# Reciprocal roots of six late norm groups: one power operation on GpSimd in place of eight VectorE steps

## The chip, the cores and the metric

The kernel runs on one core of one Trainium2 chip. The metric is the device time of one execution in microseconds (us). Executions of one kernel mostly agree within about 1%. Some are over 1.5% slower than the fastest of the same kernel, at a lower granted TensorE clock; those are called slow, and only fast runs are compared below: ratios are of fast runs alone, while a time quoted with a ratio is the median of all runs.

## The reference

Eight batches of twelve heads, sequence 512, head size 64, in float32. Rows of Q and K are divided by their norms, the scores by tau = 0.1, and then comes a softmax and the product with V.

```python
Q_norm = Q / (np.linalg.norm(Q, axis=-1, keepdims=True) + 1e-10)
K_norm = K / (np.linalg.norm(K, axis=-1, keepdims=True) + 1e-10)
scores = np.einsum('bhqd,bhkd->bhqk', Q_norm, K_norm) / tau
weights = np.exp(scores - np.max(scores, axis=-1, keepdims=True))
weights = weights / (np.sum(weights, axis=-1, keepdims=True) + 1e-10)
return np.einsum('bhqk,bhkd->bhqd', weights, V).astype(np.float32)
```

## The kernel before

The 96 heads are worked off as 48 pairs. For each pair GpSimd squares Q and K (`SQ`), sums of squares are made by TensorE and VectorE (`SSQ`, `RED`), reciprocal roots are made for a group of up to two pairs (`NEW`), Q is scaled on VectorE and K mostly on GpSimd (`SCL`), TensorE transposes (`TR`), VectorE moves the result into `qt` (`EVA`), TensorE makes the scores (`SCO`), ScalarE takes their exponentials (`EXP`, four per pair), TensorE multiplies by V (`PV`), and VectorE divides (`RCP`, `NRM`). GpSimd also converts V to bf16 (`VC`). From group 3 on, group g holds pairs 2g-3 and 2g-2.

Every engine works through a fixed list.

The roots of groups 3 to 25 take eight small VectorE steps: a first guess by integer arithmetic on the float's bits, then two rounds of improvement. The sums `xg` lie in PSUM (`n_ps`):

```python
steps = [
    lambda e: e.tensor_scalar(
        out=yg.bitcast(i32), in0=xg.bitcast(i32), scalar1=-0.5, scalar2=MAGIC,
        op0=ALU.mult, op1=ALU.add),
    yx, yyx, up(yg, 0, 2 * m), yx, yyx, up(rq_g, 0, m), up(rk_g, m, 2 * m)]
```

The squares, which the last experiments alter:

```python
P.add(("SQ", s, 0), "pool", "sq", due_sq(s), [("LD", s, 0), ("LD", s, 1)] + reds_,
      lambda e: e.tensor_tensor(out=sqf, in0=data, in1=data, op=ALU.mult))
```

Of the kernel before, what the change touches and what calls it, by code (L numbers as in the profile page):

```python
# [3 lines left out]
ALU = mybir.AluOpType  # L4
# [102 lines left out]
def bass_cosine_similarity_attention_kernel(  # L107
# [13 lines left out]
    f32, bf16, i32 = mybir.dt.float32, mybir.dt.bfloat16, mybir.dt.int32  # L121

    R_QK, R_V, R_SQ, R_QN, R_QT, R_ET, R_O, R_X = 18, 6, 6, 3, 3, 3, 8, 3

    def sb(name, shape, dt):
        return nc.alloc_sbuf_tensor(name, shape, dt)
# [11 lines left out]
    xs = {g: sb(f"xs{g}", [128, 64], f32) for g in NORM_ON_ACT}  # L138
# [3 lines left out]
    eps = sb("eps", [128, 1], f32)  # L142
    warm_in = sb("warm_in", [128, SEQ], bf16)
# [34 lines left out]
    P.add("eps", "pool", "sm_pool", -98.5, [], lambda e: e.memset(eps[:, :], 1e-19))  # L178
    P.add("table", "act", "table", -900, [], lambda e: e.preload_act_table_set("natural_log_exp_and_others"))
# [95 lines left out]
    def pair(s):  # L275
# [44 lines left out]
        acts = g in NORM_ON_ACT  # L320
# [31 lines left out]
        if s == first[g] and g in NORM_ON_ACT:  # L352
# [6 lines left out]
            P.add(("NEW", g, 6), "dve", "new", TF - 2.6, [("NEW", g, 7), ("NRMS", 0, 0, 1)],  # L359
                  lambda e: e.tensor_copy(out=n_ps[:, g % R_X, 128 : 128 + 2 * m], in_=xs[g][:, 0 : 2 * m]))  # L360
# [136 lines left out]
NORM_ON_ACT = {0: -90, 1: -45, 2: 0.5}  # L497
EARLY = 4
# [15 lines left out]
def slack(s, most):  # L514
    return most * min(1.0, s / 12)
# [4 lines left out]
        "7 8 64 65 103 104 142 143 186 11 187 221 220 105 66 263 262 296 339 338 222 297 264 372 144 188 298 373 720 "  # L520
        "679 415 830 416 417 449 450 102 491 492 374 525 63 340 526 451 721 601 493 602 645 261 754 568 567 873 831 141 "
        "949 185 797 1103 644 219 603 527 678 1137 1060 371 950 295 755 569 1102 1179 646 796 874 680 984 1289 832 1026 "
        "1025 798 907 908 909 337 875 722 1213 490 983 1366 414 448 524 1255 756 1332 1059 1104 951 1136 1442 1254 1288 "
        "1441 1061 1483 1561 985 566 1178 1331 677 1138 1365 1212 600 643 1027 1408 1407 1560 1214 753 1595 1518 829 "
        "1290 1180 719 1594 1636 1713 1671 872 1256 795 1519 1058 1517 1409 1637 1788 1670 906 1333 1484 1101 1367 982 "
        "1443 1823 948 1024 1485 1638 1562 1822 1789 1177 1596 1135 1712 1746 1330 1747 1364 1406 1672 1287 1714 1253 "
        "1211 1516 1824 1748 1635 1790 1559 1482 1669 1440 1593 1745 1711 1787 1821 1864 1865 "
    ),
    "pool": (
        "4 0 1 2 14 27 22 67 35 107 145 50 189 223 89 128 265 341 299 248 172 206 282 237 324 271 375 418 313 347 452 "  # L530
        "494 528 435 358 401 424 511 477 604 466 570 500 723 647 542 681 576 833 553 630 757 587 653 799 706 664 876 "
        "695 729 910 952 771 893 740 859 816 805 1028 882 782 1062 935 986 1105 924 958 1088 1139 1164 1257 1011 1034 "
        "1000 1181 969 1045 1334 1122 1215 1317 1240 1198 1111 1368 1153 1187 1410 1291 1229 1444 1263 1486 1427 1563 "
        "1274 1340 1520 1382 1416 1639 1351 1673 1469 1393 1458 1597 1546 1503 1656 1492 1715 1569 1749 1791 1825 1698 "
        "1611 1580 1645 1687 1721 1622 1774 1763 1732 1808 1797 1839 1851 "
    ),
    "dve": (
        "5 13 15 26 28 19 32 24 21 70 72 34 75 78 109 111 76 114 115 80 117 147 149 119 190 192 150 151 55 152 153 154 "
        "56 155 61 226 157 156 62 158 159 161 224 163 266 195 100 268 101 227 193 94 228 95 229 197 230 302 231 139 232 "
        "140 234 233 133 235 134 342 239 300 344 269 303 177 304 178 305 183 306 184 307 273 308 378 309 211 310 311 "  # L540
        "212 419 376 315 421 253 379 217 380 218 381 345 382 254 383 259 384 260 386 385 349 387 388 287 455 390 288 "
        "453 392 495 497 293 456 294 457 329 458 330 459 422 460 529 461 335 463 426 336 462 363 531 464 364 498 369 "
        "468 370 571 573 406 532 605 533 407 534 412 535 502 536 413 537 440 607 539 538 441 540 446 574 447 544 648 "
        "650 482 608 682 609 483 610 724 611 488 578 612 489 613 684 516 615 614 517 616 617 619 522 651 523 621 558 "
        "726 758 685 559 834 564 686 800 687 565 688 655 689 592 760 690 593 598 692 691 599 693 727 877 697 802 641 "
        "761 635 762 636 763 764 765 642 766 731 767 768 769 669 911 836 670 675 773 676 803 879 711 837 712 838 839 "
        "953 840 717 841 718 842 844 843 846 807 845 880 745 913 746 751 848 752 1063 850 955 787 914 788 915 793 916 "
        "794 917 918 919 987 921 920 884 922 821 989 822 827 956 828 926 1029 864 1031 990 865 991 870 992 993 871 994 "
        "1140 995 960 996 997 998 898 904 1065 899 905 1258 1106 1032 1002 1108 1066 940 1067 941 1068 946 1069 947 "
        "1070 1036 1071 1182 1072 1073 1075 974 1074 1142 975 1077 1335 1109 980 1079 981 1184 1016 1216 1143 1017 1144 "  # L550
        "1145 1146 1022 1113 1147 1023 1148 1150 1149 1050 1218 1151 1051 1369 1056 1155 1057 1185 1260 1219 1093 1220 "
        "1221 1099 1094 1222 1223 1100 1189 1224 1225 1226 1227 1292 1127 1133 1294 1128 1261 1134 1231 1445 1169 1337 "
        "1295 1170 1296 1297 1175 1298 1411 1299 1176 1300 1265 1301 1302 1203 1304 1371 1303 1204 1209 1306 1210 1487 "
        "1308 1413 1372 1245 1373 1246 1374 1338 1375 1251 1376 1252 1377 1378 1379 1342 1414 1380 1285 1279 1286 1280 "
        "1447 1564 1384 1521 1489 1322 1448 1323 1449 1450 1451 1328 1452 1329 1453 1418 1454 1455 1456 1490 1356 1523 "
        "1357 1640 1362 1460 1363 1398 1566 1399 1674 1524 1525 1598 1526 1527 1404 1528 1405 1529 1530 1494 1531 1432 "
        "1532 1600 1433 1533 1438 1535 1716 1439 1537 1642 1474 1475 1601 1602 1567 1480 1603 1604 1605 1481 1606 1571 "
        "1607 1608 1609 1643 1676 1508 1509 1613 1750 1514 1515 1718 1551 1677 1678 1679 1680 1557 1681 1682 1558 1683 "
        "1684 1552 1647 1685 1792 1585 1752 1586 1826 1591 1592 1689 1794 1627 1753 1628 1754 1755 1719 1756 1633 1757 "
        "1634 1758 1723 1760 1661 1662 1667 1759 1761 1668 1765 1795 1828 1829 1703 1830 1831 1832 1709 1704 1833 1710 "  # L560
        "1834 1836 1835 1799 1837 1737 1743 1744 1738 1841 1779 1785 1786 1780 1813 1814 1819 1820 1856 1857 1862 1863 "
    ),
    "pe": (
        "6 -256 -256 -256 -256 -256 -256 23 20 -256 -192 69 71 36 33 -128 42 38 108 43 39 110 79 46 77 48 146 148 81 "
        "116 118 83 51 52 53 54 191 85 57 58 59 87 60 225 120 90 122 96 97 124 160 162 126 91 98 99 164 267 92 93 166 "
        "196 168 135 136 137 138 194 170 301 129 130 198 131 132 200 179 180 181 182 202 236 238 204 173 343 240 174 "
        "175 176 242 272 270 244 207 208 209 210 246 377 274 213 214 215 216 276 312 249 250 314 278 251 252 420 280 "
        "316 348 255 256 257 318 258 346 320 283 284 285 322 289 290 286 454 350 291 389 292 352 391 325 326 354 327 "
        "328 496 356 393 425 331 395 359 332 333 360 397 334 361 423 399 362 530 427 365 366 467 429 367 465 368 431 "
        "402 403 404 433 405 572 408 469 409 410 501 471 411 499 473 436 437 438 439 606 475 442 443 444 503 445 505 "  # L570
        "541 543 478 507 479 480 481 649 509 575 484 545 485 486 547 512 487 577 549 513 514 515 683 551 518 519 520 "
        "579 521 581 554 618 555 556 583 620 557 725 585 560 561 622 654 562 563 624 588 652 589 626 590 591 759 628 "
        "594 595 596 597 656 658 631 632 633 637 660 638 696 694 634 662 639 801 640 698 700 728 665 666 730 702 667 "
        "671 672 704 668 835 732 770 673 674 772 734 707 708 736 709 710 878 713 738 714 804 774 715 716 741 776 742 "
        "778 806 743 747 780 744 912 748 808 749 847 750 810 783 784 785 786 812 849 954 814 789 790 791 851 792 883 "
        "853 881 817 823 855 824 825 818 819 857 826 820 988 885 925 887 860 861 923 889 862 863 1030 891 866 867 868 "
# [63 lines left out]
```

## Time and profile before

| | before |
|---|---|
| time, median of 2 runs | 192.68 us (192.58 to 192.77) |
| span of the profiled run | 189.4 us |
| VectorE (DVE) busy | 169.6 us, 90% |
| GpSimd (POOL) busy | 155.1 us, 82% |
| ScalarE (ACT) busy | 182.5 us, 96% |

From the page of before: the busy times, then three rows of the view that cuts the span into 40 slices (each digit is the busy share in tenths; PEclk is TensorE's granted clock), and the chain of waits by engine.

```profile
span 189.4 us, 6755 instructions
PE 173.9 (92%) x2729; PEld 110.3 (58%) x2729; DVE 169.6 (90%) x593; ACT 182.5 (96%) x211; POOL 155.1 (82%) x144
...
ACT  4799999999999999999999999999999999999993
POOL 5799899999999989999999978849999994516300
PEclk9999999999999999999999999999999999999999
...
ACT 93%; PE 3%; DVE 1%; POOL 1%; ACTq 0%; issue 0%; POOLq 0%
```

The exponentials are the chain. In order of time, one piece of it (start, length, what) covers nearly everything:

```profile
11.28 173.87 ACT et L445 x190
```

The recorded durations of neighbouring exponentials overlap, so ScalarE's real holds have to be read from their starts. In the trace two 128x1024 exponentials start 903 or 904 ns apart at best; I take 903.5. Over the 188 steps of the 189 large ones this makes 169.86 us; 172.26 us pass. ScalarE is held up for 2.4 us in all. I call that sum "holds" below.

### The profile page before, as it was taken

The page shows a single profiled execution, that of the slowest core. Times are in us where ns is not written, and L with a number is a line of the kernel's source. Part 1 is how long each engine was busy: PE and PEld are TensorE (multiplying, and loading weights), DVE is VectorE, ACT ScalarE, POOL GpSimd, SP SyncE. Part 2 cuts the span into 40 slices and gives each one's busy share as a digit, 9 for nine tenths or more (in the row PEclk, how much of TensorE's full clock was granted, in tenths as well). Part 3 has the DMA queues.
Part 4 walks back from the last instruction along what each step waited for, and adds up shares of the span by engine and source line. Part 5 has one row for each costly group of instructions (what it writes and reads, how often), then busy time and mean ns, then how long its engine had stood idle before and what let it go on. Part 6 is the DMA issues. An engine that isn't in the chain of part 4 may idle for free.

```text
span 189.4 us, 6755 instructions
## 1 busy us (share of the span) xinstructions
PE 173.9 (92%) x2729; PEld 110.3 (58%) x2729; DVE 169.6 (90%) x593; ACT 182.5 (96%) x211; POOL 155.1 (82%) x144
## 2 busy tenths in 40 slices
PE   5989999989999999999999899998999989999983
PEld 2645656556665665666656566565666656566552
DVE  2689999999999999999999999989999999987843
ACT  4799999999999999999999999999999999999993
POOL 5799899999999989999999978849999994516300
PEclk9999999999999999999999999999999999999999
DMA  5999999999999699999989944992249940139343
GB/s 159 349 354 349 349 350 374 363 368 370 380 383 305 177 327 374 381 351 362 378 298 295 359 162 154 316 375 84 77 144 358 290 161 21 45 106 283 111 166 111
DMA packets 52302, 50.76 MB, mean 268 GB/s; under 512 B 3120, under 2 KB 52272, under 8 KB 52272
## 3 DMA queue, kind: packets, MB, share of 16 engines
q1 hardware_dynamic: 51984, 50.08, 80.3%
q8 instruction: 21, 0.34, 0.7%
q10 hardware_dynamic: 288, 0.26, 0.4%
q14 instruction: 9, 0.07, 0.1%
HBM read 37.75 MB, written 12.58 MB: 266 GB/s over the span
## 4 chain that ended last, share of the span: by engine, by line
ACT 93%; PE 3%; DVE 1%; POOL 1%; ACTq 0%; issue 0%; POOLq 0%
ACT et L445 93%; PE ops L185 2%; PE scps L188 1%; DVE ob L476 0%; POOL vb L180 0%; ACT qt L265 0%; PE ops L330 0%; ACT ys L355 0%; ACTq L85 0%; ACT xs L357 0%; PE scps L256 0%; PE ops L459 0%; DVE rd L474 0%; POOL ident L175 0%; DVE xs L337 0%
## 5 line engine op out<-in xcount | busy, mean ns | idle before, releaser
L445 ACT ACTIVATE et<-scps 128x1024 bf16<-128x1024 f32 (+1 forms) x195 | 176.5, 1156 | 0.0
L313 POOL TENSOR_TENSOR sq<-qk 128x1024 bf16<-128x1024 f32 x45 | 84.7, 1893 | 4.6 <-DMA qk<-in_K_dram 3.6
L429 PE MATMUL scps<-qt 64*128 64x512 bf16 x384 | 75.4, 385 | 9.0 <-ACT et L445 5.3
L459 PE MATMUL ops<-vb,et 128*128 128x65 bf16 x1536 | 78.3, 194 | 0.8 <-ACT et L445 0.8
L459 PEld LDWEIGHTS ops<-vb,et 128*128 128x128 bf16 x1536 | 58.6, 98 | 29.6 <-issue 21.3
L389 POOL TENSOR_TENSOR qn<-qk,rk 128x512 bf16<-128x512 f32 x37 | 38.3, 1043 | 9.6 <-DVE rk L367 6.5
L476 DVE TENSOR_TENSOR ob<-ops,rd 128x256 f32<-128x256 f32 x96 | 39.5, 415 | 0.4
L389 DVE TENSOR_TENSOR qn<-qk,nps 128x512 bf16<-128x512 f32 x57 | 38.0, 675 | 0.1
L395 PE MATMUL tps<-ident,qn 128*128 128x128 bf16 x376 | 35.1, 220 | 0.7 <-POOL qn L389 0.5
L429 PEld LDWEIGHTS scps<-qt 64*128 64x128 bf16 x384 | 19.4, 93 | 26.8 <-ACT et L445 10.2
L402 DVE COPY qt<-tps 128x1024 bf16<-128x1024 bf16 x47 | 32.2, 685 | 3.1 <-PE tps L395 1.9
L450 POOL TENSOR_SCALAR vb<-vf 128x512 bf16<-128x512 f32 x48 | 29.3, 626 | 5.6 <-DMA vf<-in_V_dram 4.4
L341 DVE TENSOR_REDUCE nps<-sq 128x8 f32<-128x512 bf16 x44 | 29.8, 681 | 0.0
L395 PEld LDWEIGHTS tps<-ident,qn 128*128 128x128 bf16 x376 | 21.7, 98 | 11.7 <-issue 5.9
L474 DVE RECIPROCAL rd<-ops 128x4 f32<-128x4 f32 x96 | 16.6, 175 | 6.3 <-PE ops L459 5.2
L330 PE MATMUL ops<-sq,ident 128*128 128x64 bf16 x400 | 19.7, 193 | 0.0
L330 PEld LDWEIGHTS ops<-sq,ident 128*128 128x128 bf16 x400 | 14.9, 98 | 3.4 <-issue 2.3
L337 DVE TENSOR_REDUCE nps<-ops 128x8 f32<-128x64 f32 x46 | 9.9, 217 | 1.0 <-PE ops L330 0.9
L362 DVE TENSOR_TENSOR nps<-nps,ys 128x32 f32<-128x32 f32 (+1 forms) x46 | 8.8, 191 | 0.3
L363 DVE SCALAR_TENSOR_TENSOR nps<-nps,ys 128x32 f32<-128x32 f32 (+1 forms) x46 | 8.7, 190 | 0.3
L185 PE MATMUL ops<-warm_in,ident 128*128 128x512 bf16 x8 | 3.6, 631 | 2.0 <-POOL eps L178 2.0
L367 DVE SCALAR_TENSOR_TENSOR nps<-nps,ys 128x16 f32<-128x16 f32 (+1 forms) x30 | 5.1, 171 | 0.1
(43 smaller groups left out, 36.2 us busy)
## 6 DMA issues: line engine op xcount, KB each, us to landing
vf<-in_V_dram SPq DMA_DIRECT2D x48, 256.0 KB, 6.0
qk<-in_Q_dram SPq DMA_DIRECT2D x47, 256.0 KB, 6.0
qk<-in_K_dram SPq DMA_DIRECT2D x47, 256.0 KB, 6.1
out_dram<-ob SPq DMA_DIRECT2D x47, 256.0 KB, 5.1
qk<-in_K_dram ACTq DMA_DIRECT2D x2, 128.0 KB, 2.9
qk<-in_Q_dram SPq DMA_DIRECT2D x2, 128.0 KB, 2.7
out_dram<-ob SPq DMA_DIRECT2D x2, 128.0 KB, 1.7
```

The source lines that it names most:

```text
L313: lambda e: e.tensor_tensor(out=sqf, in0=data, in1=data, op=ALU.mult))
L330: last = e.matmul(out=o_ps[bank][:, 320:384], lhsT=ident[:, :], rhs=sq[iqs][:, 8 * w : 8 * w + 8, 8 * k : 8 * k + 8], start=(k == 0), stop ...
L341: lambda e, w=w, dst=dst: e.tensor_reduce(out=dst, in_=sq[iqs][:, 8 * w : 8 * w + 8, :], axis=AX.X, op=ALU.add))
L389: lambda e, w=w, r=r: e.tensor_tensor(out=qn[iqn][:, w].rearrange("p t h d -> p h t d"), in0=qk[iq][:, w].rearrange("p h (t d) -> p h t d" ...
L395: last = e.transpose(t_ps[:, w, t, :], qn[iqn][:, w, t].rearrange("p h d -> p (h d)"), ident[:, :])
L402: lambda e: e.tensor_copy(out=qt[iqt][:, :, :, :].rearrange("p w t x -> p (w t x)"), in_=t_ps[:, :, :, :].rearrange("p w t x -> p (w t x)")))
L429: last = e.matmul(out=sc_ps[:, 2 * b + h, :], lhsT=qt[iqt][64 * h : 64 * h + 64, 1, c, :], rhs=qt[iqt][64 * h : 64 * h + 64, 0, :, :], sta ...
L445: lambda e, c=c, b=b, hs=hs: e.activation(out=et[iet][:, c, hs[0] : hs[-1] + 1, :], in_=sc_ps[:, 2 * b + hs[0] : 2 * b + hs[-1] + 1, :], f ...
L450: lambda e: e.tensor_scalar(out=vb[:, iq, :, :, 0:DIM].rearrange("p c h d -> p h c d"), in0=vf[iv][:, :, :].rearrange("p h (c d) -> p h c ...
L459: last = e.matmul(out=o_ps[h][:, 65 * t : 65 * t + 65], lhsT=et[iet][:, c, h, 128 * t : 128 * t + 128], rhs=vb[:, iq, c, h, :], start=(c = ...
L474: lambda e, h=h, grid=grid: e.reciprocal(out=rd[io][:, h, :], in_=grid[:, :, DIM]))
L476: lambda e, h=h, grid=grid: e.tensor_tensor(out=ob[io][:, h], in0=grid[:, :, 0:DIM], in1=rd[io][:, h, :].unsqueeze(2).to_broadcast([128, N ...
```

## The change

It is meant to relieve VectorE: for six late groups the sums go to SBUF, GpSimd adds a tiny constant and raises to the power -0.5, and VectorE only copies the result into PSUM. The orders of all engines and of the DMA queue were searched anew. The core of the diff:

```diff
-    xs = {g: sb(f"xs{g}", [128, 64], f32) for g in NORM_ON_ACT}
+    xs = {g: sb(f"xs{g}", [128, 64], f32) for g in (*NORM_ON_ACT, *NORM_ON_POOL)}
+    mhalf = sb("mhalf", [128, 1], f32)
+    P.add("half", "pool", "sm_pool", -97, [], lambda e: e.memset(mhalf[:, :], -0.5))
-        acts = g in NORM_ON_ACT
+        acts = g in NORM_ON_ACT or g in NORM_ON_POOL
+        elif s == first[g] and g in NORM_ON_POOL:
+            P.add(("NEW", g, 0), "pool", "sm_pool", TF - 5.8 - slack(s, M_NEW), reds,
+                  lambda e: e.tensor_scalar(
+                      out=xs[g][:, 0 : 2 * m], in0=xs[g][:, 0 : 2 * m], scalar1=1e-19, scalar2=1.0, op0=ALU.add, op1=ALU.mult))
+            P.add(("NEW", g, 7), "pool", "pow", TF - 5.5 - slack(s, M_NEW), [("NEW", g, 0), "half"],
+                  lambda e: e.tensor_tensor(
+                      out=xs[g][:, 0 : 2 * m], in0=xs[g][:, 0 : 2 * m], in1=mhalf[:, :].to_broadcast([128, 2 * m]), op=ALU.pow))
+            P.add(("NEW", g, 6), "dve", "new", TF - 2.9 - slack(s, M_NEW), [("NEW", g, 7), *free[0], *free[1]],
+                  lambda e: e.tensor_copy(out=n_ps[:, g % R_X, 128 : 128 + 2 * m], in_=xs[g][:, 0 : 2 * m]))
+NORM_ON_POOL = (11, 14, 17, 20, 23, 24)
...  # ORDER: every engine's list replaced
```

## The prediction

> **What bounds it now.** ScalarE. In the chain that ended last, the exponentials (L445) hold 92.6%; one unbroken piece of 190 runs from 11.28 us for 173.87 us. The page shows ACT idle 0.0, but recorded durations overlap (median 1168 ns), so I read starts from the trace: neighbouring 128x1024 exponentials start 903.5 ns apart at best (median 904). From first to last start of the 189 large ones 172.26 us pass; 188 steps at 903.5 ns would need 169.86. So ScalarE is held up for only 2.4 us in all, about 1.2 us of it after 72 us, where the changed groups lie. VectorE is busy 169.6 us (90%), GpSimd 155.1 us (82%); neither matters to the chain between 12 and 185 us. By windows, GpSimd is nearly full until 108 us, busy 8.9 to 9.8 of 12 us from 108 to 132, full to 156, and 5.2 to 5.5 of 12 us from 156 to 180.
>
> **The change.** Groups 11, 14, 17, 20, 23, 24 each drop eight VectorE steps on at most 128x32 (188, 192, 191, 183, 192, 191, 172, 161 ns in the groups view: 1.47 us) and gain one copy (like L360, 0.18 us): 6 x 1.29 = 7.7 us off VectorE, 90% to 86%. Sums of squares go to SBUF, since GpSimd cannot access PSUM (the Trainium skill, "GPSIMD Engine Reference", section 1; this trace agrees: no GpSimd line touches a PSUM tile). GpSimd gains an add of about 0.15 us and a power per group. All orders, DMA too, are re-searched.
>
> **Cost of the power.** The trace doesn't measure it, no page states it. Section 3.1 of that page has long GpSimd bodies bound at about 3 operations per cycle; some 50 operations on 32 elements would be about 0.5 us, a dependent chain several us. The diff allows 2.6 us between the power's due time and the copy's. My estimate: 2.3 us, plausibly 0.8 to 6. Six cost 14 us: GpSimd goes to about 170 us.
>
> **Critical path.** Before, roots are ready 2.4 to 3.1 us after the last sum for these groups (1.8 for group 23), since the steps interleave with other VectorE work. Add plus power plus copy with semaphores: about 2.8 us. So latency is unchanged, and VectorE's relief can be cashed only in the 1.2 us of late ScalarE holds. I expect 0.2 to 0.5 us gained there, as much won or lost by the new order elsewhere. Slack before harm: from the copy into qt (L402) to its pair's first exponential 0.8 to 2.4 us (about 0.6 needed), and from scaling to that copy 1 to 3 us. A power above roughly 4.5 us would use this up and stall in-order VectorE at the copy; each excess us would cost up to 6 us in all.
>
> **Predicted time** 192.5 us, 191.4 to 195.0. Faster by over 2% (below 188.8) is practically impossible: removing every ScalarE hold gives about 190.3. Chances 0.01, 0.87, 0.12.
>
> **What would show it.** Exponentials still above 92% of the chain, 903.5 ns start to start, holds summing to 1.5 to 3 us; VectorE busy 162 us, GpSimd 170 us; power group x6 at 2.3 us; first exponential within 0.3 us of 9.27.
>
> **What would make it wrong.** A power far longer than 2.3 us, or a code load at first use: then holes between exponentials in pairs 19, 25, 31, 37, 43, 45, with VectorE waiting at the new copy. A re-searched DMA order that starves GpSimd's squares. Contention of GpSimd and VectorE on SBUF; the trace shows none now (square 1889 to 1902 ns throughout).

## More of the kernel before

The order is a table of numbers, and before each entry the engine waits on semaphores for what that entry needs. So whatever stands behind a waiting entry waits too:

```python
for o in order[name]:
    ... # collect the highest value wanted of each semaphore
    for k, (sem, val) in want.items():
        engine.wait_ge(sem, val)
    inst = o.emit(engine)
    if o.sem is not None:
        inst.then_inc(o.sem, o.inc)
```

The groups of instructions that the change and the argument touch (busy us, mean ns of one, then idle time of the engine before them and its releaser):

```profile
L445 ACT ACTIVATE et<-scps 128x1024 bf16<-128x1024 f32 (+1 forms) x195 | 176.5, 1156 | 0.0
L313 POOL TENSOR_TENSOR sq<-qk 128x1024 bf16<-128x1024 f32 x45 | 84.7, 1893 | 4.6 <-DMA qk<-in_K_dram 3.6
L429 PE MATMUL scps<-qt 64*128 64x512 bf16 x384 | 75.4, 385 | 9.0 <-ACT et L445 5.3
L362 DVE TENSOR_TENSOR nps<-nps,ys 128x32 f32<-128x32 f32 (+1 forms) x46 | 8.8, 191 | 0.3
L363 DVE SCALAR_TENSOR_TENSOR nps<-nps,ys 128x32 f32<-128x32 f32 (+1 forms) x46 | 8.7, 190 | 0.3
```

The small steps of the roots take some 0.19 us each by duration; a square takes ten times that.

## The result

The change took 220.09 us (two runs, 220.05 and 220.14) against 192.68 us: a ratio of 1.1423, 95% interval 1.1374 to 1.1472. Results are correct.

The same views of the page of after:

```profile
span 217.9 us, 6727 instructions
PE 186.2 (85%) x2729; PEld 117.3 (54%) x2729; DVE 166.4 (76%) x551; ACT 185.2 (85%) x211; POOL 189.2 (87%) x157
...
ACT  4799999998999965999579993799947999466993
POOL 4799989879999999999999979997999799989100
PEclk9999999999999996999769997699976999769999
...
ACT 40%; PE 24%; POOL 21%; DMA 6%; DVE 5%; issue 2%; SPq 2%; ACTq 0%; POOLq 0%
...
L456 ACT ACTIVATE et<-scps 128x1024 bf16<-128x1024 f32 (+1 forms) x195 | 179.2, 1086 | 25.5 <-PE scps L440 25.1
L440 PE MATMUL scps<-qt 64*128 64x512 bf16 x384 | 79.2, 405 | 10.3 <-ACT et L456 5.2
L315 POOL TENSOR_TENSOR sq<-qk 128x1024 bf16<-128x1024 f32 x45 | 84.6, 1895 | 3.4 <-DMA qk<-in_K_dram 2.2
L368 POOL TENSOR_TENSOR xs<-xs,mhalf 128x32 f32<-128x32 f32 x6 | 32.6, 5429 | 0.2
L371 DVE COPY nps<-xs 128x32 f32<-128x32 f32 x6 | 1.2, 195 | 20.1 <-POOL xs L368 20.1
```

Read it from the bottom. One power on 128x32 takes 5.43 us (5426 to 5437 ns for all six, the first included), and VectorE stands idle for 20.1 us in front of the six copies. ScalarE's row has five dents, the last of them long and from two powers, and the clock's row falls to 6 or 7 tenths in the same five places. Those are means over slices of 5.4 us: the windows view gives a granted clock of 0.50 from 82.5 to 85.8 us and again from 106.4 to 113.1 us, and 1.00 between. The holds, from the starts of the exponentials, are 30.6 us instead of 2.4. The chain is no longer ScalarE's alone.

The first power in the timeline of after (start, length, engine, line, operation; in brackets the idle time before and its releaser). The cuts are of GpSimd, VectorE, TensorE and ScalarE, in this order, in the same stretch:

```profile
74.58 0.22 POOL L365 TENSOR_SCALAR xs<-xs 128x32 f32<-128x32 f32 x1
74.88 0.63 POOL L461 TENSOR_SCALAR vb<-vf 128x512 bf16<-128x512 f32 x1
75.47 5.44 POOL L368 TENSOR_TENSOR xs<-xs,mhalf 128x32 f32<-128x32 f32 x1
...
80.94 0.20 DVE L371 COPY nps<-xs 128x32 f32<-128x32 f32 x1 [3.48 <-POOL xs L368]
...
78.08 0.39 PE L440 MATMUL scps<-qt 64*128 64x512 bf16 x2 [0.43 <-ACT et L456]
...
81.91 0.40 PE L406 MATMUL tps<-ident,qn 128*128 128x128 bf16 x4 [3.21 <-DVE qn L400]
82.72 0.61 PE L440 MATMUL scps<-qt 64*128 64x512 bf16 x2
...
83.36 1.02 ACT L456 ACTIVATE et<-scps 128x1024 bf16<-128x1024 f32 x1 [3.50 <-PE scps L440]
```

The wait is handed from queue to queue. VectorE stops at the copy for 3.48 us; TensorE stops at the transposes of pair 19, which stand in its list ahead of the last scores of pair 18; ScalarE runs dry for 3.50 us. Then the same two score products take 0.61 us instead of 0.39.

### The profile page after: what moved, and what is told of

Same layout as the page of the kernel before. It is cut to its first block, busy times and chain, and to the rows that moved or that the text cites. A ratio compares the mean times of both kernels' runs of the same rounds, so it can differ in the third digit from the quotient of the medians.

```text
span 217.9 us, 6727 instructions
## 1 busy us (share of the span) xinstructions
PE 186.2 (85%) x2729; PEld 117.3 (54%) x2729; DVE 166.4 (76%) x551; ACT 185.2 (85%) x211; POOL 189.2 (87%) x157
## 4 chain that ended last, share of the span: by engine, by line
ACT 40%; PE 24%; POOL 21%; DMA 6%; DVE 5%; issue 2%; SPq 2%; ACTq 0%; POOLq 0%
ACT et L456 39%; POOL xs L368 15%; PE scps L440 9%; PE ops L470 8%; PE tps L406 4%; DMA qk<-in_K_dram 3%; POOL sq L315 3%; PE ops L332 2%; DMA qk<-in_Q_dram 2%; POOL vb L461 1%; DVE qt L413 1%; SPq L291 1%; POOL qn L400 1%; DVE qn L400 1%; DVE ob L487 1%
## 5 line engine op out<-in xcount | busy, mean ns | idle before, releaser
L456 ACT ACTIVATE et<-scps 128x1024 bf16<-128x1024 f32 (+1 forms) x195 | 179.2, 1086 | 25.5 <-PE scps L440 25.1
L440 PE MATMUL scps<-qt 64*128 64x512 bf16 x384 | 79.2, 405 | 10.3 <-ACT et L456 5.2
L315 POOL TENSOR_TENSOR sq<-qk 128x1024 bf16<-128x1024 f32 x45 | 84.6, 1895 | 3.4 <-DMA qk<-in_K_dram 2.2
L470 PE MATMUL ops<-vb,et 128*128 128x65 bf16 x1536 | 82.1, 199 | 3.9 <-DVE ob L487 3.2
L470 PEld LDWEIGHTS ops<-vb,et 128*128 128x128 bf16 x1536 | 62.0, 101 | 35.4 <-issue 22.6
L440 PEld LDWEIGHTS scps<-qt 64*128 64x128 bf16 x384 | 19.5, 93 | 28.4 <-ACT et L456 9.3
L406 PEld LDWEIGHTS tps<-ident,qn 128*128 128x128 bf16 x376 | 23.1, 102 | 20.1 <-DVE qn L400 9.9
L368 POOL TENSOR_TENSOR xs<-xs,mhalf 128x32 f32<-128x32 f32 x6 | 32.6, 5429 | 0.2
L400 POOL TENSOR_TENSOR qn<-qk,rk 128x512 bf16<-128x512 f32 x25 | 26.0, 1045 | 6.2 <-DVE rk L378 6.2
L343 DVE TENSOR_REDUCE nps<-sq 128x8 f32<-128x512 bf16 x32 | 21.6, 681 | 0.0
L371 DVE COPY nps<-xs 128x32 f32<-128x32 f32 x6 | 1.2, 195 | 20.1 <-POOL xs L368 20.1
L400 POOL TENSOR_TENSOR qn<-qk,xs 128x512 bf16<-128x512 f32 x12 | 12.4, 1043 | 0.1
L339 DVE TENSOR_REDUCE nps<-ops 128x8 f32<-128x64 f32 x34 | 7.4, 221 | 2.9 <-PE ops L332 2.7
L343 DVE TENSOR_REDUCE xs<-sq 128x8 f32<-128x512 bf16 x12 | 8.1, 674 | 0.4 <-POOL sq L315 0.4
```

Of the source, the lines that this page charges most:

```text
L343: lambda e, w=w, dst=dst: e.tensor_reduce(out=dst, in_=sq[iqs][:, 8 * w : 8 * w + 8, :], axis=AX.X, op=ALU.add))
L368: lambda e: e.tensor_tensor(out=xs[g][:, 0 : 2 * m], in0=xs[g][:, 0 : 2 * m], in1=mhalf[:, :].to_broadcast([128, 2 * m]), op=ALU.pow))
L400: lambda e, w=w, r=r: e.tensor_tensor(out=qn[iqn][:, w].rearrange("p t h d -> p h t d"), in0=qk[iq][:, w].rearrange("p h (t d) -> p h t d" ...
L406: last = e.transpose(t_ps[:, w, t, :], qn[iqn][:, w, t].rearrange("p h d -> p (h d)"), ident[:, :])
L440: last = e.matmul(out=sc_ps[:, 2 * b + h, :], lhsT=qt[iqt][64 * h : 64 * h + 64, 1, c, :], rhs=qt[iqt][64 * h : 64 * h + 64, 0, :, :], sta ...
L456: lambda e, c=c, b=b, hs=hs: e.activation(out=et[iet][:, c, hs[0] : hs[-1] + 1, :], in_=sc_ps[:, 2 * b + hs[0] : 2 * b + hs[-1] + 1, :], f ...
```

## The experiments

Theory L: latency. A power keeps an in-order queue for longer than the schedule tolerates, and the wait travels to ScalarE. Theory W: work. GpSimd has no time left for 33 us more. Theory O: the new orders are slow by themselves. Theory C: TensorE's lower clock behind each hold makes part of the loss. In the texts written before each run, A is the power's duration as a whole (with A1 for L by way of VectorE's copy, A2 for W), B is O, and G is L told of GpSimd's own queue.

An attempt not run: the power on VectorE, in one step for every group. It did not compile (the same step with a multiplication did), so that version could not be tried.

### The orders without the power: e1_mult

```diff
-    memset(mhalf[:, :], -0.5)   ...   op=ALU.pow
+    memset(mhalf[:, :], 1.0 / 512)   ...   op=ALU.mult
```

> The changed kernel with its orders untouched, but the power replaced by a multiplication by 1/512 of the same shape (results wrong on purpose, values near the right ones). It takes away the power's duration alone. Theory A (the duration of the power, 5.43 us x6, makes the loss): the kernel falls from 220.1 to 192 to 195 us, with only the hold of about 2 us at 36 to 41 us that a late DMA makes in the changed order. Theory B (the re-searched orders are bad by themselves): it stays above 205 us. The multiplication should take about 0.25 us.

Measured: 192.1 us, ratio 0.9992 (0.9952 to 1.0031), wrong results. From its page and its view of the tile `mhalf` (minimum, median, maximum ns):

```profile
PE 174.9 (92%) x2729; PEld 110.8 (58%) x2729; DVE 165.5 (87%) x551; ACT 182.5 (96%) x211; POOL 158.0 (83%) x157
...
L368 POOL TENSOR_TENSOR xs<-xs,mhalf x6: 239/240/244, 73.9 to 167.9; 128x32 f32<-128x32 f32 x6
```

Theory O falls: the searched orders are as good as those of before, and all of the loss is the power's 5.43 us in place of 0.24. The run says something else too: VectorE is relieved, and nothing is gained. Holds are 2.8 us. There was next to nothing for this change to win: all holds before come to 2.4 us.

### The power's work without its result: e2_idle_ahead and e2_idle_behind

Both are the kernel before with six powers on a constant tile; nobody reads the output.

```diff
+    for g in (11, 14, 17, 20, 23, 24):
+        P.add(("POW", g), "pool", "pow", 0, ["half", "pin"], lambda e: e.tensor_tensor(
+            out=p_out[:, :], in0=p_in[:, :], in1=mhalf[:, :].to_broadcast([128, 32]), op=ALU.pow))
     # order: ahead of the scaling of K of the group's first pair / behind that of its second pair
```

> The kernel before, with six powers of the same shape added on GpSimd whose result nobody reads, each just ahead of the scaling of K of the group's first pair, where the changed kernel has its own. VectorE keeps its eight steps and never waits for a power. Theory A1 (the loss comes through VectorE, which waits in order at the copy): small loss, but the scalings of K behind the power come 5.4 us late, so some loss is left, 200 to 212 us. Theory A2 (occupancy of GpSimd alone: 33 us more work): about as slow as the change, 215 to 222 us.

> As the run before, but each idle power stands just behind the scaling of K of the group's second pair, so that only squares, conversions of V and later scalings queue behind it. GpSimd has the same 33 us more work. If occupancy is what costs (A2): as slow as with the powers ahead, over 210 us. If only what waits directly behind a power costs: 193 to 200 us.

Measured: 221.68 us (ratio 1.1538) ahead, 222.03 us (1.1515) behind. Both lose at least as much as the change, though VectorE waits for no power. The low forecasts (A1, 200 to 212 us, and 193 to 200 us) were wrong; those by occupancy came true, as they would by any theory that blames GpSimd's queue. In the run with the powers behind, the waits view names other victims: the squares, the scalings of K and the conversions of V that stand behind a power.

```profile
DVE nps L344 <- POOL sq L316: 9.8, 3, 5.3
PEld tps L398 <- POOL qn L392: 9.8, 5, 4.4
PEld ops L462 <- POOL vb L453: 9.5, 2, 4.9
```

(Engine and what waited, for whom, us in total, times, longest.) The longest single waits are 4.4 to 5.3 us. The constant input takes 5.43 us as well, so the duration was the same for the two kinds of data tried.

### The power cut by pair: e3_pairs

The changed kernel, but only the first pair's 16 columns are raised at once; the second pair's power, copy, scaling of Q and transposes stand later in the lists.

```diff
-  power on all 32 columns; copy of all 32
+  power on columns of pair 1; copy of those; ...; power on columns of pair 2; copy of those
```

> The changed kernel with each power cut in two by pair: first the 16 columns of the group's first pair, whose copy follows at once; then, behind the scaling of K of that pair, the 16 of the second, whose copy, scaling of Q and transposes are moved later. Correct results, same GpSimd work. If the duration is in proportion to the elements, each half takes about 2.8 us. Theory A1 (latency of the power before the first pair): the hold of ScalarE at the first pair shrinks by about 2.6 us in each of six groups and the kernel falls to 200 to 208 us. Theory A2 (occupancy): it stays at 215 to 221 us.

Measured: 222.97 us, ratio 1.1599, correct. VectorE's wait at the first copies fell from 20.1 to 9.8 us, yet nothing was won: holds are 32.7 us. TensorE's transposes waited 14.9 us for VectorE's scalings instead of 9.9. From the waits views, two lines of this run and one of after:

```profile
DVE nps L375 <- POOL xs L372: 9.8, 6, 5.3
PEld tps L411 <- DVE qn L405: 14.9, 11, 5.8
...
PEld tps L406 <- DVE qn L400: 9.9, 6, 3.3
```

A half takes 2.90 us. That spoke for W, but the edit also moves the second pair's work close to where it is needed, so it is no clean test.

### How long may it take: e4_2us and e4_3us

Stand-ins of chosen length for the power, in the changed kernel; results are wrong.

```diff
+            def stand_in(e):
+                for i, n in enumerate(PAD):   # (512, 512) or (512, 512, 512)
+                    e.tensor_tensor(out=pad[:, ..., 0:n], in0=warm_in[:, 0:n], in1=warm_in[:, 0:n], op=ALU.mult)
+                return e.tensor_tensor(...)   # the multiplication of e1_mult
```

> The changed kernel with each power replaced by a stand-in of about 2.3 us, the duration that the prediction had estimated: two 128x512 products of a constant tile (about 1.04 us each) and then the multiplication by 1/512 of e1_mult (0.24 us); results wrong on purpose. If only the size of the power was wrong in the prediction: within 1% of before (190.5 to 194.5 us). If the tolerance of the order is what was wrong, i.e. under 2 us: 196 to 204 us.

> As e4_2us with three products, about 3.4 us for each stand-in. The prediction had put the threshold at about 4.5 us, so by it nothing is lost (191 to 195 us). In the changed kernel's trace the first hold after a power of 5.43 us is about 3.4 us, so the order tolerates about 2 us: by that, 1.4 us and a tail are lost six times, 200 to 206 us.

Measured, from the start of the first product to the end of the last operation:

| time in place of the power | 0.24 us (e1_mult) | 2.23 us | 3.23 us | 5.43 us (the change) |
|---|---|---|---|---|
| ratio to before | 0.9992 | 1.0100 | 1.0473 | 1.1423 |
| VectorE's idle before the copies | 0.0 us | 3.5 us | 9.1 us | 20.1 us |
| holds of ScalarE | 2.8 us | 4.4 us | 13.4 us | 30.6 us |

The copies in the groups views of e1_mult, e4_2us and e4_3us:

```profile
L371 DVE COPY nps<-xs 128x32 f32<-128x32 f32 x6 | 1.1, 182 | 0.0
...
L376 DVE COPY nps<-xs 128x32 f32<-128x32 f32 x6 | 1.2, 195 | 3.5 <-POOL xs L368 3.4
...
L376 DVE COPY nps<-xs 128x32 f32<-128x32 f32 x6 | 1.2, 195 | 9.1 <-POOL xs L368 9.1
```

At the length that I had estimated the kernel takes 194.4 us, inside the predicted range. The tolerance is near 2 us, not 4.5. Above 3.23 us each microsecond on six powers costs 0.095 x 192.7 / 2.20 = 8.3 us in all, more than the six that it adds.

### The same work in small pieces: e5_chopped

```diff
-  6 idle powers of 32 columns (5.43 us)
+  32 idle powers of 4 columns (1.0 us), spread evenly over GpSimd's list from pair 20 on
```

> The kernel before with 32 idle powers of 4 columns each (about 1.0 us each, 32 us in all, as much GpSimd work as the six of 5.43 us) spread evenly over the GpSimd order from pair 20 on; nobody reads them. Theory G (the long block in an in-order queue costs): GpSimd was idle for 19.5 us between 72 and 180 us, so about 13 us at most is lost, 195 to 206 us, with no holds over 2 us and the TensorE clock at 1.0. Theory W (total work of GpSimd costs): as slow as the six blocks, 215 to 223 us.

Measured: 215.32 us, ratio 1.1175. Theory L alone would have most of the loss vanish. It doesn't. The page shows GpSimd at eight or nine tenths in every slice from the fifth to the 34th, which ends at 182 us:

```profile
POOL 5797999999999899999999999899999999476500
```

By windows it was idle for 1.2 us of the 96 us from 84 to 180 us; the kernel before was idle there for 19.5 us. Work added, 32.6 us, less the 19.5 us makes 13 us; 22.6 us were lost.

### One power, in a gap and in a busy stretch: e6_one_in_gap and e6_one_in_busy

```diff
+  one idle power behind the scaling of K of pair 42 (gap) / of pair 20 (busy), in the kernel before
```

> The kernel before with a single idle power of 5.43 us, placed where GpSimd sat idle 3.3 us in the trace of before (behind the scaling of K of pair 42, at 158.6 us). It then delays the next scaling by about 2.1 us. If a block costs only what it overlaps beyond the idle time and the tolerance of the order: 0 to 1.5 us. If every power costs about 4.7 us wherever it stands: 196 to 198 us.

> The kernel before with one idle power of 5.43 us behind the scaling of K of pair 20, where GpSimd was full (72 to 108 us). A sixth of what six such powers cost (29 us): 4.5 to 5.5 us, so 197 to 198.5 us, against 1.0 us (fast runs) in the place where GpSimd was idle. If the place makes no difference: about 194 us.

Measured on fast runs: ratio 1.0050 (1.0006 to 1.0095, 1 us) in the gap, 1.0250 (1.0204 to 1.0295, 4.8 us) in the busy stretch. Half of the runs of the first were slow ones. In this gap, on the fast half of the runs, a power cost a fifth. The slow half took 196.5 to 197.1 us at clocks of 0.988 to 0.991, while none of the eleven runs of before beside them was slow. Whether the power itself brings that on, so that a fifth is too little, was not tested.

### Latency alone and GpSimd relieved: e8_late_copy and e7_half_squares

```diff
 # e8: e1_mult, and the copy needs a later GpSimd entry too (as ("VC", 20) for group 11)
-  [("NEW", g, 7), *free[0], *free[1]]
+  [("NEW", g, 7), LATE[g], *free[0], *free[1]]
 # e7: the changed kernel
-  out=sqf, in0=data, in1=data
+  out=sqf[:, 0:n_sq], in0=data[:, 0:n_sq], in1=data[:, 0:n_sq]     # n_sq = 512 from pair 20 on
```

> e1_mult (multiplication of 0.24 us for the power, results wrong on purpose), but VectorE's copy of the roots also waits for a GpSimd operation that stands 2.7 to 5.2 us of work further on in its order. GpSimd does no more work than in e1_mult (192.1 us); only the latency to VectorE is that of the changed kernel. Theory L: VectorE waits about 3 us at each copy and most of the loss is there, 208 to 220 us. Theory W: under 198 us.

> The changed kernel, power and all, but from pair 20 on GpSimd squares only half of each tile (512 of 1024 columns; results wrong on purpose): 28 squares shorter by 0.85 us, 24 us less GpSimd work, nothing else altered. Theory W (GpSimd has no time left, so work added is time added): most of the loss comes back, 195 to 203 us. Theory L (the latency of the power in the chain to VectorE's copy): the copy still waits 3 us or more six times, 212 to 220 us.

Measured: 211.46 us, ratio 1.0921, for the late copy; 216.79 us, ratio 1.1241, with halved squares. Without any added work, latency to VectorE costs about 18 us. With GpSimd's busy time down to 165.5 us the change still loses 24 us, and its copies still wait 19.8 us:

```profile
PE 183.9 (86%) x2729; PEld 115.8 (54%) x2729; DVE 165.7 (77%) x551; ACT 184.6 (86%) x211; POOL 165.5 (77%) x157
...
DVE nps L373 <- POOL xs L370: 19.8, 6, 3.6
```

So W alone falls as well.

### Two by two: e10_before_half, e10_chopped_half, e10_block_half

Long blocks or pieces, with GpSimd full or with halved squares from pair 20 on (the edit of e7 on before, e5_chopped and e2_idle_behind).

> Control: the kernel before with half-width squares from pair 20 on (results wrong on purpose), GpSimd relieved by 24 us and no power. ScalarE bounds, so the same time as before, within 1%: 191 to 194 us.

> e5_chopped (32 idle powers of 1.0 us, 215.3 us) with half-width squares from pair 20 on. Each piece is shorter than the tolerance of about 2 us, and GpSimd has 24 us of the 33 us back. If full GpSimd time is what e5_chopped lost by: 193 to 199 us. If even short pieces cost by delaying what follows: over 205 us.

> e2_idle_behind (six idle powers of 5.43 us, 222 us) with half-width squares from pair 20 on. If the length of one block costs whatever GpSimd's total is: 208 to 218 us, far above the pieces. If total work is all: the same as the pieces, 193 to 199 us.

| ratio to before | full squares | squares halved from pair 20 |
|---|---|---|
| no power | 1 | 0.9995 |
| 32 idle pieces of 1.0 us | 1.1175 | 1.0225 |
| 6 idle blocks of 5.43 us | 1.1515 | 1.1055 |

Short pieces on a relieved GpSimd cost 4 us; long blocks on the same GpSimd cost 20 us; short pieces on a full one cost 23 us. Either cause by itself makes most of the loss, and the two do not add up. Only with both taken away does it nearly go; the 4 us left (1.0174 to 1.0276) are clear of noise and not explained. The rows of GpSimd and of the clock in slices, first of the pieces and then of the blocks, both with halved squares:

```profile
POOL 5699799999999766999999999959999998648300
PEclk9999999999999999999999999999999999999998
```

```profile
POOL 5799999999995569959799464998699848638900
PEclk9999999999999999969966999999999999789978
```

With blocks, GpSimd has idle slices again, and time is lost all the same.

### TensorE kept busy through the hold: e9_fill and e11_fill_placed

```diff
+        for k in range(40):
+            last = e.transpose(t_ps[:, 0, k % NT, :], ident[:, :], ident[:, :])
     # e9: ahead of the group's first transposes; e11: ahead of what waits longest in the trace of after
```

> The changed kernel with 40 dummy transposes (into a bank that the next transposes overwrite) ahead of the first transposes of each of the six groups, so that TensorE works through the hold behind a power instead of idling. In the changed kernel the products behind each hold take 0.61 us instead of 0.39 and the steps of ScalarE 1.3 to 1.7 us for some 3 us. If idling lowers the granted clock and that costs: clock back to above 0.98, 6 to 9 us won, 211 to 214 us. If the clock is no cause: 219 to 221 us.

> The changed kernel with 40 dummy transposes (2.4 us at full clock) just ahead of the TensorE instruction that waits longest behind the power, in groups 11, 14, 17, 20 and 23, as read from its trace. If idling lowers the granted clock and the slow products behind the hold cost: clock above 0.97, steps of ScalarE behind the hold back near 0.9 us, 4 to 8 us won, 212 to 216 us. If not: 219 to 221 us.

Measured: e9_fill 223.67 us (ratio 1.1583), a miss. Its trace shows why: in groups 14, 17 and 24 TensorE had stopped at other entries before it came to the dummies, and then did 3.73, 3.49 and 4.10 us of them behind the hold. The mean clock still rose to 0.966, and no time was won (some 3 us were lost), so a better mean clock is no gain by itself. Placed right in five groups, 215.68 us (1.1208, 1.1129 to 1.1286), against 1.1423 for the change: some 4 us won, at a mean clock of 0.981 in the profiled run instead of 0.930. The score products come back to 390 ns (405 in after, 385 in before); the clock's row of e11_fill_placed and its line from the groups view:

```profile
PEclk9999999999999999999999999999999999995898
...
L440 PE MATMUL scps<-qt 64*128 64x512 bf16 x384 | 76.4, 390 | 11.7 <-ACT et L456 4.8 <-DVE qt L413 4.2 <-DVE ob L487 0.4
```

Theory C holds for about a sixth of the loss, as far as this filling takes it away, and net of what the dummies themselves cost. The Trainium skill, "TensorE: Matmul & The Clock Gate", section "HAM oscillation — how this bites in real kernels", warns of TensorE idling for more than about 3.4 us; here a hold of 2.66 us between products (group 14, in the timeline of after) was already followed by products of 0.61 us. The length alone does not decide: after a hold of 2.22 us in the same trace (to 199.36 us) products took 0.39 us, while after one of 1.81 us in e3_pairs (to 84.45 us) they took 0.61 us from 85.59 us on.

## Why the prediction was wrong

1. ScalarE bounds the kernel and a relief of VectorE cannot be cashed: right. With the cheap stand-in the time is that of before (0.9992).
2. "6 x 1.29 = 7.7 us off VectorE": the sum of durations was right, the effect was not. Over all VectorE instructions of the trace the durations add up to 207.3 us in before and 199.6 us in e1_mult, 7.7 us less; busy time, in which an overlap counts once, fell from 169.6 to 165.5 us, by 4.1 us. The Trainium skill, "Perfetto Trace Analysis", section "Optimizing Scalar/DVE Operations", says of the fixed overhead of an operation that its profiled latency is about twice the time that it keeps the engine busy, since half of it overlaps with the next instruction; 7.7 against 4.1 us, for small steps, agrees with that.
3. "My estimate: 2.3 us, plausibly 0.8 to 6": the power took 5.43 us, inside the wide range and 2.4 times the centre. This is the term of the sum that was mis-sized. Six of them took 32.6 us instead of 14 and brought GpSimd to 189.2 us, not 170. With 2.23 us in its place the kernel stayed in the range. I took the centre from the due times in the diff, which are somebody's plan and no measurement.
4. "A power above roughly 4.5 us would use this up": this step was wrong by itself, and it kept the range narrow. 2.23 us cost 1%, 3.23 us cost 4.7%. It is the larger fault: with the measured 5.43 us put into this rule, (5.43 - 4.5) x 6 = 5.6 us are lost, about 198 us in all, and 220.1 us were measured. I had added up slack along one path, from the roots of a pair to its own exponential. But the lists are in order: behind the copy stand VectorE's divisions, behind the transposes stand the scores of the pair before, and behind the power stand squares and conversions of V. In the trace of after, the first hold starved pair 18's scores while pair 19's roots were late.
5. "Each excess us would cost up to 6 us in all": too little. It was 8.3 us between 3.23 and 5.43 us. A lower clock behind each hold is one added cost, shown at about 4 us; what makes up the rest was not told apart.
6. The first symptoms listed for being wrong came true: holds at the first pairs of the six groups, VectorE waiting at the new copy. The other suspects did not show: the first power was as short as the rest, the squares took 1895 ns against 1893, and GpSimd idled 3.4 us in front of them against 4.6. Not listed was that GpSimd's own queue would lose as much without anybody waiting for the power. I had only checked that 170 us of GpSimd work fit into the span. The pieces show that its idle time isn't free, and the blocks on a relieved GpSimd show that even idle time does not help against one long entry.

Open: 32.6 us of pieces less 19.5 us of idle time explain 13 of the 22.6 us that e5_chopped lost; I did not split the rest between waits and clock. Also open is whether orders searched with 5.43 us as the power's cost would do better. They could win little over before, since all holds there come to 2.4 us, and in the one order tried even 0.24 us in place of the power gave 0.9992; no version that beats both kernels was found.

## What to carry to other kernels

Before work is moved to another engine, measure the new operation there alone; a plan built on a guess for it is worth the guess. In a schedule of in-order queues ask two things of the receiving engine: has it time for the sum of the work in that stretch, and does the longest single entry fit the tolerance of everything behind it. Here either one sufficed for most of the loss, and relieving a busy engine that is not the bound gained nothing.

## What the Trainium skill lacked or had wrong

- "GPSIMD Engine Reference" has no figure for a power. The runs show 1.01 us for 128x4, 2.90 us for 128x16 and 5.43 us for 128x32 in float32, that is about 0.16 us per column plus 0.4 us, where a multiplication of 128x32 takes 0.24 us. Its rule of about 3 operations per cycle for long bodies (section 3.1) gives a time only with the number of operations, and the 50 that I put in were a guess.
- "TensorE: Matmul & The Clock Gate" puts the harmful gap at about 3.4 us. Here a gap of 2.66 us between products was followed by products of 0.61 instead of 0.39 us, and a gap of 1.81 us in e3_pairs was too, but not one of 2.22 us in after.
- "Perfetto Trace Analysis" says that half of the fixed overhead in a profiled latency overlaps with the next instruction; it has no number for steps taken out of a chain like this one. 42 fewer VectorE operations took 4.1 us off the busy time (e1_mult), about 0.1 us each, though each lasts about 0.19 us in the trace.
